# The largest magnitude of a weight strip, spread over the partitions by TensorE and VectorE in place of GpSimd

## The chip, the core and the metric

The kernel runs on one core of one Trainium2 chip. The metric is the device time of one execution in microseconds. Engines are named as in the profile: PE is TensorE's products, PEld its weight loads, DVE is VectorE, ACT is ScalarE, POOL is GpSimd and SP is the engine that only issues DMAs.

## The reference

One inference step of a decoder trunk of two layers, width 1024: a state-space layer and a gated linear recurrence, each followed by a feed-forward layer. There are 1040 prompt tokens (16 of them meta tokens) and 8 sample tokens. Norms, convolutions and recurrences stand around the products; the products with weights carry the arithmetic:

```python
h = rms_norm(x, p["norm_mix_pre"][i])
m, c_new, s_new = ssd_mixer(h, ...)     # or rglru_mixer
x = x + rms_norm(m, p["norm_mix_post"][i])
h = rms_norm(x, p["norm_ffn_pre"][i])
x = x + rms_norm(sq_relu_mlp(h, p["ffn_w1"][i], p["ffn_w2"][i]), p["norm_ffn_post"][i])

def sq_relu_mlp(x, w1, w2):
    h = jax.nn.relu(x @ w1)
    return (h * h) @ w2
```

All inputs are float32, and the products must come out close to float32.

## The kernel before, in words

**Products in float16 parts.** A float32 operand is scaled by a power of two and split into a high and a low float16 part. A product is three passes on PE: high by high, high by low, low by high. Tokens lie along the free dimension in three chunks of 350, 350 and 348 columns.

**Weights come in strips.** A strip is 1024 rows by 256 columns, 1 MB. `wlane` (L399) walks through a list of 113 strips as a generator, one step per `tick`, beside the products. A strip is loaded by SP into one of two buffers `ws` (`load_strip`, L257). Then `wconv` (L285) makes its scale and its parts:

- `rm`, one number per partition that bounds the strip's values there. For kind a it is a sum of magnitudes that ACT accumulates; for kinds d, h and H it is a VectorE reduction over 2048 columns; for kinds 2 and S VectorE reduces in two halves to `r4`, weighs them and reduces again; kind s takes a column that kind g stored in `gmx`.
- `strip_scale` (L262) takes the largest of the 128 numbers on every partition, `wgb`, by GpSimd's `partition_all_reduce`, and VectorE makes from it, in one-column operations, the power of two (`qw`, `pw`, `sw`) and its inverse `winv`.
- ACT writes the high part into `wh`, VectorE the low part (`split`, L271). For kinds H and S (`sums`, L349) there are also the parts `wp` of some quarters, and GpSimd forms four sums of quarters in place in `ws`, which are then split in turn.
- for the first product of a feed-forward layer `hidden_scale` (L418) makes from `wgb` a scale of the hidden units; it multiplies the bound by 32.0.

**Wide and narrow products.** The state-space layer, the recurrent layer and the first and last products of each feed-forward layer are plain (`bundle`): 24 products of 350 or 348 columns per output tile. In between, the feed-forward products go by Winograd's form (`unit`, L1350): seven products of quarters, of 175 or 174 columns, into four of eight PSUM banks, and VectorE adds them up in `z`. The sums of quarters of activations (`f`, `TT`, `HT`) are made by GpSimd (`input_sums`, `t_sums`). `mm` (L240) hands out the banks in turn, eight in the feed-forward layers, four within the state-space groups.

**What sets the order.** The scheduler of the language orders each engine's instructions from the order in which the kernel issues them and from its own estimate of times; on the chip each engine then runs its row in order, waiting at each instruction for its operands. The first 100 us are an exception: in `start` (L746) the engines `hold` the written order. Most operations pass through the wrapper class `Queue`, so that the profile gives L89 (or L92, in the held part) as the line of nearly all; tiles tell them apart.

Of the kernel before, what the change touches and what calls it, by code (L numbers as in the profile page):

```python
# [11 lines left out]
F16 = mybir.dt.float16  # L12
I32 = mybir.dt.int32
AF = mybir.ActivationFunctionType
OP = mybir.AluOpType
AX = mybir.AxisListType
PSUM = bass.MemoryType.PSUM
DRAM = bass.MemoryType.DRAM
# [3 lines left out]
P = 128  # L22
D = 1024
KT = 8
# [29 lines left out]
def cols(c):  # L54
    """The columns of a chunk of tokens."""
    return slice(c * CW, c * CW + WC[c])


class Carve:
    """Small float32 tiles cut from larger ones."""  # L60
# [17 lines left out]
class Queue:  # L78
    """An engine; while hold is set its instructions are issued in program order, and later ones behind them."""
# [38 lines left out]
class Body:  # L118
# [7 lines left out]
    # ------------------------------------------------------- order of work  # L126
    def tick(self):
        """One step of every piece of work that runs beside the matrix products."""
        for lane in list(self.lanes):
            if next(lane, self) is self:  # L130
                self.lanes.remove(lane)
# [5 lines left out]
    def tab(self, *args, **kw):  # L137
        """An activation whose function needs a table set: these stay in program order."""
        if self.last_tab is None or self.nc.scalar.hold:
            self.last_tab = self.nc.scalar.activation(*args, **kw)  # L140
        else:
            with self.tc.issue_after(self.last_tab.ins):
                self.last_tab = self.nc.scalar.activation(*args, **kw)
# [8 lines left out]
    # ---------------------------------------------------------------- setup  # L152
    def setup(self):
# [28 lines left out]
        # pre-norm gains and group-norm gains scaled by a power of two so that hi/lo fit float16  # L182
# [13 lines left out]
        # the inputs of the ffn leave room for sums of four  # L196
# [48 lines left out]
    def pow2(self, b, n, pool, tag):  # L245
        """p = the power of two at or below b; s = 2^14 / p."""
# [9 lines left out]
    # -------------------------------------------------------------- weights  # L256
# [5 lines left out]
    def strip_scale(self, gmax):  # L262
        nc, ty = self.nc, self.tiny
        gb = ty.tile([P, 1], F32, tag="wgb", name="wgb")
        nc.gpsimd.partition_all_reduce(gb, gmax, P, RED.absmax)
        s, p = self.pow2(gb, 1, ty, "w")
        inv = ty.tile([P, 1], F32, tag="winv", name="winv", bufs=8)
        nc.vector.tensor_scalar(inv, p, 2.0 ** -14, None, op0=OP.mult)
        return s, inv, gb

    def split(self, w, st, s, parts):  # L271
        """w = float16 hi and lo parts of st * s, s [P, parts] by contiguous column ranges."""
# [12 lines left out]
    def wconv(self, st, kind, cols=SW):  # L285
        """A strip of weights as float16 hi and lo parts [P, 2, KT, cols], the factor that undoes its scaling and,
        for kinds h and H, the factor of its hidden units. Kind a takes a bound from the sums of the magnitudes, kind s
        one that kind g found before; kinds 2 and S carry the factors of the hidden rows. Kinds H and S are for the
        products by Winograd's form: with the quarters that are used as they are."""
# [50 lines left out]
    def quarter(self, s, inv):  # L340
        """Scales that leave room for sums of four."""
# [7 lines left out]
    def sums(self, wp, st, s, npair, parts):  # L349
        """Steps: the quarters of a strip [K tiles, M] that are used as they are, A11, A12, A22 (A ij: m tile i, k  # L350
        tiles of parity j), as float16 parts in wp; then the sums of Winograd's form in the room of the strip. Only
        the first npair pairs of k tiles."""
# [20 lines left out]
    def product(self, ps, i, w, B, T, npair):  # L373
        """ps = one of the seven products of quarters over the first pairs of k tiles, three passes of the float16
        parts; open for the products of the other pairs where there are any."""
# [14 lines left out]
    def quadrant(self, w, B, npair, i, l):  # L390
        """The operands of m tile i by half l of the tokens over the other pairs."""
# [26 lines left out]
    def hidden_scale(self, wmax, inv):  # L418
        """The factors of one strip's hidden units: t = 2^7, or 2^6 where the squares are summed, / (power of two at or
        below the bound on the values before the square, the norm of the input times that of a column); returns  # L420
        t / (scales of the product); 1 / t^2 goes to rj."""
# [6 lines left out]
        nc.vector.tensor_scalar(lb, wmax, self.gbound[:, gi:gi + 1], 32.0, op0=OP.mult, op1=OP.mult)  # L428
# [14 lines left out]
    def summed(self, b, s):  # L443
        """Whether the hidden units of a strip of block b enter the second product by Winograd's form."""
        return b < 3 and s < NSUM
# [6 lines left out]
    def bundle(self, ps, w, m, act, c, kts=range(KT), first=True, last=True):  # L452
        """ps += sum over k of w[k, m tile]^T act[k, chunk c], three passes of the float16 parts."""
# [14 lines left out]
    def new_u(self):  # L468
        """Float16 parts of the normed input by chunk and k tile."""
# [4 lines left out]
    def u_rows(self, U, c):  # L474
        """The bytes of chunk c of U as float32 rows."""
        return U[:, c].bitcast(F32).rearrange("p k s c -> p k (s c)")

    # ---------------------------------------------------------------- norms
    def rstd(self, sumsq, n, pool, w):
        """1 / sqrt(mean + eps) on every partition, from per-partition sums of squares."""  # L480
# [17 lines left out]
    def normed(self, x, ss, i, hi, lo, pool):  # L498
        """Steps: the pre-norm i of a chunk (its k tiles in x), as float16 parts in hi and lo [P, KT, n]."""
# [15 lines left out]
    def boundary(self, m, ss, xc, piece, ipost, xdst, ipre, U, pool):  # L515
        """Steps: x + norm(m) for a piece of a chunk to xdst; then its pre-norm."""
# [37 lines left out]
    def last_phase(self, ws, act, ipost, xsrc, xdst, ipre, evac, pre=None, split0=None):  # L554
        """The last product before a norm, chunk by chunk; the norms of a chunk run beside the next one."""
# [47 lines left out]
    def first_phase(self, strips, act, evac):  # L603
        """Products of the first strips after a norm: chunk 2 of the input comes last."""
# [15 lines left out]
    # ------------------------------------------------------------------ SSD  # L620
# [67 lines left out]
    def start_x(self, c):  # L688
        """A chunk of the input, in the room of later rows: its k tiles, and room left over."""
# [25 lines left out]
    def start_norm(self, U, c, x, sq, ufs):  # L715
        """Steps: the first pre-norm of a chunk."""
# [29 lines left out]
    def start(self, U):  # L746
        """The first pre-norm beside the first products, issued in this order."""
# [20 lines left out]
    def dt_phase(self, U, dts, dtt, w):  # L768
        """Step sizes, decays and their cumulative sums, tokens on partitions: columns (tile, head); tiles 0-7
        are the chunks of the prompt, 8 the meta tokens, 9 the sample tokens."""  # L770
# [31 lines left out]
        # the sums again, tokens along the rows, in DRAM, from where they are spread over the partitions  # L802
# [22 lines left out]
        # sample tokens  # L825
# [3 lines left out]
        # head rows by sample, then spread over the partitions of the features  # L829
# [13 lines left out]
    def softplus(self, out, x, pool, n, parts=1):  # L843
        """max(x, 0) + log1p(exp(-|x|)), the logarithm by the series of 2 artanh(e / (2 + e)); by parts of the
        columns that don't wait for each other."""
# [23 lines left out]
    def evac_ext(self, pre, ps, c, inv, bias=0.0):  # L869
        """A chunk of projected columns into the layout of the convolution: 8 x (3 state + 1), 3 zeros, tokens."""  # L870
# [10 lines left out]
    def conv_tile(self, pre, out, w4, b1, cvo):  # L881
        """Depthwise convolution of width 4; the last three columns of each sequence go to cvo [P, 27]."""
# [16 lines left out]
    def proj_x(self, g, start=False):  # L899
        """Projection and convolution of the x, B and C columns of a group."""  # L900
# [84 lines left out]
    def ssd_group(self, g):  # L985
# [26 lines left out]
        def spread(i):  # L1012
            """The cumulative sums of a chunk's tokens on every partition."""
# [68 lines left out]
        def sample_bc():  # L1082
            """B and C of the sample tokens, by way of DRAM, on every partition."""
# [22 lines left out]
        def sample_b(b2):  # L1106
            """Two sample tokens: h += x B and y = h C, B and C spread over the partitions."""
# [45 lines left out]
    def group_norm(self, g):  # L1153
        """Steps: gate, norm within the group, float16 parts."""
# [25 lines left out]
    def half_a(self):  # L1180
        """The first half of the output projection, kept in DRAM by chunks."""
# [43 lines left out]
    # ------------------------------------------------------------------ FFN  # L1225
    def ffn(self, l):
# [8 lines left out]
        for b in range(4):  # L1235
# [3 lines left out]
            def square(c, s, r):  # L1239
                """The squares of r (m tile, half of the tokens) as float16 parts, and their sums."""  # L1240
# [78 lines left out]
    def t_sums(self, f, t1, t234):  # L1319
        """Steps: the sums of quarters of the right operand for Winograd's form, in their room in f (B jl: k tiles of  # L1320
        parity j, half l of a chunk's tokens, the last half first): T1 = B12 - B11, T2 = B22 - T1, T3 = B22 - B12,
        T4 = B21 - T2, and their float16 parts."""
# [9 lines left out]
    def input_sums(self, U, TT, fp):  # L1332
        """Steps: the sums of quarters of the input, T1 in the room of B12 and the others in TT."""
# [16 lines left out]
    def unit(self, w, BT, c, npair, fp):  # L1350
        """Two m tiles by a chunk, [C12, C11, C22, C21] (C il: m tile i, half l of the tokens, the last half first), the
        first pairs of k tiles by Winograd's form: seven products of quarters."""
# [27 lines left out]
    # ------------------------------------------------------------------ LRU  # L1380
    def lru(self):
# [99 lines left out]
        # a bound on |h gate|: (32.3 max|x| + max|h0|) (norm of u times that of a column of weights + max|b|)  # L1481
# [74 lines left out]
def _strips(w, ns):  # L1556
    """[K, N] as [ns, 128, (K / 128) * (N / ns)], each strip contiguous per partition."""
# [4 lines left out]
def _fm(x):  # L1562
    """[..., n * 128] as [128, n, ...]"""
# [95 lines left out]
```

## Time and profile before

| | us |
|---|---|
| median of 3 runs | 2842.84 (2841.06 to 2843.44) |
| span of the profiled execution | 2836.7 |
| PE busy in it | 2583.1 |
| VectorE busy | 2110.1 |
| ScalarE busy | 1322.6 |
| GpSimd busy | 691.4 |

The profiled execution's own time isn't listed apart from the runs; its span, from the first instruction to the last, is 2836.7 us, and the three runs lie 4.4 to 6.7 us above it. In the profile's rows `x` is a count; the number in brackets, or behind the bar in groups, is the time that the engine stood idle just before, with what ended it. "issue" there means that nothing in the profile was being waited for.

### The profile page before, as it was taken

How to read it: one execution, taken by the hardware profiler on the slowest of the kernel's cores; microseconds unless marked ns; L12 is line 12 of the kernel's file. 1: busy time of each engine (PE TensorE's matmuls, PEld its weight loads, DVE VectorE, ACT ScalarE, POOL GpSimd, SP SyncE). 2: the span in 40 equal slices, each digit the busy share in tenths (PEclk: the TensorE clock that was granted, in tenths of full speed). 3: DMA queues.
4: the chain of work that ended last, by engine and by line, in shares of the span. 5: the costliest groups of instructions: out<-in, count | busy, mean ns of one | idle time of the engine just before them, and what ended most of it. 6: DMA issues, size and time to landing. Idle time of an engine off the chain costs nothing. (4 is left out here: it accounts for less than half of the span.)

```text
span 2836.7 us, 56933 instructions
## 1 busy us (share of the span) xinstructions
PE 2583.1 (91%) x23209; PEld 2060.6 (73%) x23209; DVE 2110.1 (74%) x5043; ACT 1322.6 (47%) x2148; POOL 691.4 (24%) x972
## 2 busy tenths in 40 slices
PE   4999999999999999789989999979999779989998
PEld 2666666666666667789989976646667779989976
DVE  4889778977873685568778788787685667878776
ACT  4655455545544354344253344658564335253352
POOL 2222111212212024442232201123014452231301
PEclk9999999999999999889999999989999989999999
DMA  3232233223345320101122123110220101111122
GB/s 123 99 119 90 87 107 115 102 88 108 113 159 187 117 106 31 46 31 46 61 72 79 46 110 113 63 62 33 89 108 31 46 31 46 47 45 53 54 73 95
DMA packets 52758, 229.15 MB, mean 81 GB/s; under 512 B 9056, under 2 KB 18416, under 8 KB 31632
## 3 DMA queue, kind: packets, MB, share of 16 engines
q1 hardware_dynamic: 46112, 190.81, 19.1%
q0 software_dynamic: 6384, 34.71, 3.1%
q8 instruction: 181, 2.97, 0.4%
q14 instruction: 81, 0.66, 0.1%
HBM read 186.28 MB, written 39.22 MB: 79 GB/s over the span
## 5 line engine op out<-in xcount | busy, mean ns | idle before, releaser
L89 PEld LDWEIGHTS <-wh 128*128 128x128 f16 x17040 | 1504.0, 99 | 503.7 <-issue 54.7
L89 PE MATMUL mm<-U,wh 128*128 128x350 f16 (+3 forms) x7056 | 989.4, 297 | 20.7 <-ACT rr L89 13.2
L89 PE MATMUL mm<-H,wh 128*128 128x175 f16 (+5 forms) x5664 | 557.7, 253 | 35.3 <-DVE z L89 30.4
L89 PEld LDWEIGHTS <-wp 128*128 128x128 f16 x3888 | 311.0, 99 | 87.6 <-issue 60.5
L89 POOL TENSOR_TENSOR ws<-ws 128x256 f32<-128x256 f32 (+1 forms) x192 | 205.2, 1069 | 328.6 <-DVE wp L89 214.4
L89 DVE TENSOR_TENSOR z<-z,mm 128x175 f32<-128x175 f32 (+3 forms) x648 | 228.4, 370 | 29.2 <-ACT z L89 22.0
L89 POOL PARTITION_ALL_REDUCE wgb<-rm x100 | 55.5, 555 | 656.6 <-issue 338.4
L89 PE MATMUL mm<-U,wp 128*128 128x175 f16 (+1 forms) x1728 | 154.8, 245 | 55.2 <-DVE z L89 55.1
L89 PE MATMUL mm<-TT,wh 128*128 128x175 f16 (+1 forms) x1728 | 167.0, 248 | 10.2 <-ACT TT L89 9.3
L89 ACT ACTIVATE z<-z,ti 128x700 f32<-128x700 f32 (+1 forms) x72 | 63.0, 875 | 183.5 <-DVE z L89 183.5
L89 DVE SCALAR_TENSOR_TENSOR wh<-ws,sw,wh 128x1024 f16<-128x1024 f32 x94 | 122.0, 1320 | 28.3 <-ACT wh L89 28.3
L89 DVE TENSOR_SCALAR qw<-wgb 128x1 f32<-128x1 f32 x103 | 15.5, 150 | 167.3 <-POOL wgb L89 167.1
L89 DVE SCALAR_TENSOR_TENSOR wh<-ws,s,wh 128x256 f16<-128x256 f32 x256 | 114.7, 490 | 11.1 <-ACT wh L89 11.1
L89 DVE TENSOR_REDUCE rm<-ws 128x1 f32<-128x2048 f32 x40 | 91.3, 2281 | 31.2 <-DMA ws<-w 26.7
L89 PE MATMUL mm<-H,wp 128*128 128x175 f16 (+1 forms) x864 | 90.5, 241 | 25.5 <-DVE z L89 23.1
L89 DVE TENSOR_TENSOR ss<-ss,sqt 128x350 f32<-128x350 f32 (+3 forms) x154 | 75.9, 500 | 41.8 <-ACT sqt L89 41.1
L89 ACT ACTIVATE wh<-ws,s 128x512 f16<-128x512 f32 x128 | 83.0, 710 | 48.0 <-POOL ws L89 23.2
L89 DVE SCALAR_TENSOR_TENSOR conv<-pre,ssmall,conv 128x1072 f32<-128x1072 f32 x78 | 103.8, 1330 | 0.1
L89 ACT ACTIVATE wh<-ws,sw 128x2048 f16<-128x2048 f32 x47 | 93.7, 1993 | 14.5 <-DVE sw L89 11.7
L89 DVE TENSOR_SCALAR L<-L,ncs 128x128 f32<-128x128 f32 (+1 forms) x288 | 90.6, 357 | 13.2 <-DMA L<-csd 13.2
L89 DVE TENSOR_TENSOR H<-z,H 128x175 f16<-128x175 f32 (+5 forms) x120 | 81.2, 694 | 23.6 <-ACT H L89 19.5
L89 ACT ACTIVATE pre<-mm,undo 128x8 f32<-128x8 f32 (+1 forms) x104 | 46.5, 474 | 110.7 <-PE mm L89 110.7
(279 smaller groups left out, 4176.9 us busy)
## 6 DMA issues: line engine op xcount, KB each, us to landing
ws<-w SPq DMA_DIRECT2D x64, 1024.0 KB, 4.9
ws<-w_ssd_in SPq DMA_DIRECT2D x24, 1024.0 KB, 5.4
L<-csd SPq DMA_DIRECT2D x64, 256.0 KB, 3.2
ws<-w_lru_in SPq DMA_DIRECT2D x12, 1024.0 KB, 4.9
xd<-xc POOLq DMA_DIRECT2D x6, 1400.0 KB, 5.5
xc<-xd SPq DMA_DIRECT2D x6, 1400.0 KB, 6.0
h<-ssd_h SPq DMA_DIRECT2D x8, 1024.0 KB, 4.9
bc<-bcd SPq DMA_DIRECT2D x8, 1024.0 KB, 4.8
```

The lines of the kernel that those rows point to most:

```text
L89: r = f(*args, **kw)
```

## The change

In `strip_scale` the call on GpSimd goes. In its place PE multiplies: the stationary operand is the upper half of `rm` as bfloat16 (its float32 bytes without the last 16 bits), repeated over 128 columns, and the moving operand is the identity, also as bfloat16. Each output partition then holds all 128 numbers in a row, in a PSUM bank from `mm`, and VectorE reduces that row by its maximum. The bits that are cut off make the maximum smaller by up to 1 in 128, and the bound in `hidden_scale` takes 32.3 in place of 32.0. 109 all-reduces are replaced so; the two others, of the norms' gains (`gb`) and of a bound in the recurrent layer (`gx`), stay on GpSimd. Comments were removed too, so line numbers move by up to five: L89 and L92 become L90 and L93.

```diff
+BF16 = mybir.dt.bfloat16
...
     def strip_scale(self, gmax):
         nc, ty = self.nc, self.tiny
+        ps = self.mm()
+        nc.tensor.matmul(ps[:, :P], gmax.bitcast(BF16)[:, 1:2].to_broadcast([P, P]), self.ident.bitcast(BF16)[:, 1::2], start=True, stop=True)
         gb = ty.tile([P, 1], F32, tag="wgb", name="wgb")
-        nc.gpsimd.partition_all_reduce(gb, gmax, P, RED.absmax)
+        nc.vector.tensor_reduce(gb, ps[:, :P], axis=AX.X, op=OP.max)
         s, p = self.pow2(gb, 1, ty, "w")
...
-        nc.vector.tensor_scalar(lb, wmax, self.gbound[:, gi:gi + 1], 32.0, op0=OP.mult, op1=OP.mult)
+        nc.vector.tensor_scalar(lb, wmax, self.gbound[:, gi:gi + 1], 32.3, op0=OP.mult, op1=OP.mult)
```

The scheduler also orders every engine anew. Three places show it. On POOL, in the first feed-forward layer, while the activations' sums `f` and the weights' sums `ws` are made, there stood before:

```order
L89 TENSOR_TENSOR f<-U 128x350 x2
L89 TENSOR_TENSOR f<-f 128x175 x2
L89 ISA
L89 ISA wgb<-rm 128x1
L89 ISA
L89 TENSOR_TENSOR f<-f 128x175
```

and now:

```order
L90 TENSOR_TENSOR f<-U 128x350 x2
L90 TENSOR_TENSOR f<-f 128x175 x4
L90 TENSOR_TENSOR ws<-ws 128x2x128 x4
L90 TENSOR_TENSOR f<-U 128x350 x2
L90 TENSOR_TENSOR f<-f 128x175 x4
```

The all-reduce went, and with it the instructions without operands that stood ahead of it and behind it.

On VectorE, at a strip of the second hidden block (`z` adds up products, `H` and `HT` are parts of hidden units), the reduction `rm` over a whole strip stood before among these:

```order
L89 TENSOR_REDUCE rm<-ws 128x1
L89 TENSOR_TENSOR z<-z,mm 128x175
L89 TENSOR_TENSOR H<-z,H 128x175
L89 TENSOR_TENSOR H<-z,H 128x350
L89 TENSOR_TENSOR z<-mm,z 128x2x175
L89 TENSOR_TENSOR z<-z,mm 128x175
L89 TENSOR_TENSOR z<-z,mm 128x2x175
L89 TENSOR_TENSOR z<-z,mm 128x175
L89 TENSOR_SCALAR qw<-wgb 128x1
```

and now among these:

```order
L90 TENSOR_TENSOR z<-z,mm 128x2x175
L90 TENSOR_TENSOR H<-z,H 128x174
L90 TENSOR_REDUCE rm<-ws 128x1
L90 TENSOR_TENSOR HT<-z,HT 128x3x174
L90 TENSOR_TENSOR z<-z,mm 128x175
L90 TENSOR_REDUCE wgb<-mm 128x1
L90 TENSOR_TENSOR z<-z,mm 128x175
L90 TENSOR_SCALAR qw<-wgb 128x1
```

Between `rm` and the use of the maximum there stood five `z` adds; one stands there now, and the reduction of the bank is new. On PE the product with `rm` stands between the products for that `z` add and the next ones.

On SP, in a group of the state-space layer, the weight loads `ws` and the loads `L` of decay sums for VectorE stood before:

```order
L1017 DMA L<-csd 128x512
L259 DMA ws<-w_ssd_in 128x2048 x3
L1017 DMA L<-csd 128x512
L1090 DMA bcd_143<-row 8x256
L1093 DMA bc<-bcd_143 128x2048
L1017 DMA L<-csd 128x512 x6
```

and now:

```order
L1022 DMA L<-csd 128x512
L260 DMA ws<-w_ssd_in 128x2048 x2
L1022 DMA L<-csd 128x512
L1095 DMA bcd_143<-row 8x256
L1098 DMA bc<-bcd_143 128x2048
L1022 DMA L<-csd 128x512 x3
L260 DMA ws<-w_ssd_in 128x2048
L1022 DMA L<-csd 128x512 x2
```

The third weight load moved back by four `L` loads.

## The prediction

> **What bounds the kernel now.** I read the table of busy time first, then the same table by stretches of the program.
>
> ```profile
> span 2836.7 us, 56933 instructions
> PE 2583.1 (91%) x23209; PEld 2060.6 (73%) x23209; DVE 2110.1 (74%) x5043; ACT 1322.6 (47%) x2148; POOL 691.4 (24%) x972
> 0.00:140.00 140.00, 96.68 (x802) 63.92 (x803) 95.92 (x197) 74.19 (x111) 41.79 (x63) 0.95 0.31 111
> 140.00:1094.57 954.57, 914.02 (x6073) 630.62 (x6072) 730.03 (x1949) 469.15 (x733) 188.48 (x314) 0.98 0.32 113
> 1094.57:1668.40 573.83, 508.21 (x6266) 497.15 (x6263) 425.76 (x1058) 230.69 (x405) 179.22 (x233) 0.95 0.16 56
> 1668.40:2166.90 498.50, 472.44 (x3033) 308.67 (x3033) 382.81 (x655) 293.75 (x444) 92.67 (x116) 0.98 0.21 77
> 2166.90:2737.19 570.29, 503.46 (x6267) 493.08 (x6264) 415.54 (x1050) 227.79 (x400) 178.57 (x233) 0.95 0.14 48
> 2737.19:2836.70 99.51, 88.30 (x776) 67.19 (x776) 60.04 (x138) 27.07 (x57) 10.65 (x13) 0.97 0.24 86
> ```
>
> Columns are length, then busy time of PE, PEld, DVE, ACT, POOL, then the granted clock. PE is the bound and is idle for 253.6 us. The densest idle time lies in the first 140 us (43.3) and in the two feed-forward stretches of Winograd units (65.6 and 66.8), where the clock is also lowest, 0.95. The waits say who is late.
>
> ```profile
> POOL wgb L89 <- issue: 338.4, 56, 9.3
> DVE qw L89 <- POOL wgb L89: 167.1, 68, 11.7
> PE mm L89 <- DVE z L89: 113.2, 70, 6.2
> POOL ws L89 <- issue: 96.1, 14, 10.2
> ```
>
> GpSimd stands 338.4 us ahead of 56 of its all-reduces although no operand is missing, 6.0 us each, and 96.1 us ahead of 14 weight sums. VectorE stands 167.1 us in 68 waits for the all-reduce. PE's largest wait is for VectorE's `z` adds, which free its banks. One place of the timeline joins the three (first number start, second duration, bracket the idle time ahead):
>
> ```profile
> 1103.02 0.36 POOL L89 PARTITION_ALL_REDUCE wgb<-rm  x1 [4.56 <-DVE rm L89]
> 1110.35 1.53 POOL L89 TENSOR_TENSOR f<-U 128x350 f32<-128x350 f16 x2 [6.97 <-issue]
> 1111.95 2.35 POOL L89 TENSOR_TENSOR f<-f 128x175 f32<-128x175 f32 x4
> 1113.50 0.42 DVE L89 TENSOR_TENSOR U<-f,U 128x175 f16<-128x175 f32 x1 [6.14 <-ACT U L89]
> 1116.98 2.77 PE L89 MATMUL mm<-H,wh 128*128 128x174 f16 x18 [2.43 <-DVE z L89]
> ```
>
> The call takes 0.36 us; the next ordinary GpSimd operation starts 6.97 us later with nothing awaited. VectorE loses 6.14 us to it, PE 2.43 us. The order rows of POOL above show what stands there. The all-reduce and the operand-less instruction on each side of it go. Rows of operand-less instructions fall from 167 to 7 in the program. I read them as the change of GpSimd's code, since the 6 to 7 us lie exactly there. The Trainium skill (GPSIMD Engine Reference, 4.1 Engine selection) advises GpSimd for reductions along partitions. By its 0.36 us call alone the change would have nothing to gain; the rows on both sides of the call decide against that.
>
> **The change part by part.** *The two unit stretches* hold 12,528 narrow products. What they can run at is shown by slices of 100 us and by undisturbed rows:
>
> ```profile
> 1100.00:1200.00 100.00, 81.50 (x959) 79.49 (x959) 58.02 (x151) 33.06 (x65) 48.05 (x71) 0.91 0.09 33
> 1200.00:1300.00 100.00, 82.75 (x945) 81.08 (x944) 67.80 (x163) 46.14 (x76) 43.92 (x61) 0.87 0.09 33
> 1300.00:1400.00 100.00, 97.38 (x1269) 96.07 (x1267) 81.94 (x213) 33.34 (x65) 22.16 (x24) 1.00 0.16 54
> 1400.00:1500.00 100.00, 85.54 (x1049) 83.30 (x1047) 74.81 (x179) 49.23 (x85) 31.62 (x44) 0.95 0.21 75
> 1500.00:1600.00 100.00, 95.97 (x1235) 93.37 (x1234) 82.46 (x212) 26.28 (x51) 22.04 (x23) 1.00 0.18 65
> 2167.36 0.62 PE L89 MATMUL mm<-HT,wh 128*128 128x175 f16 x6
> 2167.82 0.62 PE L89 MATMUL mm<-H,wh 128*128 128x175 f16 x6
> ```
>
> The floor is 0.46 us for six, 76.7 ns. The good slices give 78.8 (100 us / 1269) and 81.0 ns, and these still contain all-reduces; the bad ones 104 to 106. The stretches together take 573.8 + 570.3 = 1144.1 us, 91.3 ns each. I take 81.5 ns, just above the good slices, because VectorE is already 82% busy in them: 1021.0 us, **-123**. Bounds: -157 at 78.8 ns, -183 at the floor, and the VectorE case under the rivals.
>
> *Added on PE:* 109 products of 128 columns. The trace has no such float16 product. Its bounds:
>
> ```profile
> 77.58 6.15 PE L92 MATMUL mm<-wh,U 128*128 128x32 f16 x240
> 390.18 0.49 PE L89 MATMUL tp<-ident,conv 128*16 128x128 f32 x3
> L89 DVE TENSOR_TENSOR cbm<-cb,tri 128x128 f32<-128x128 f32 x64 | 17.8, 277 | 0.0
> L89 DVE TENSOR_REDUCE rm<-ws 128x1 f32<-128x2048 f32 x40 | 91.3, 2281 | 31.2 <-DMA ws<-w 26.7 <-DMA ws<-w_lru_out 2.5 <-DMA ws<-w_lru_in 1.8
> ```
>
> These are 26 ns at 32 columns and 163 ns for a float32 product with the identity; I take 0.1 us, between them: 64 in the feed-forward layers, most of them in the units, **+6**; 32 in the state-space part, +3; 12 in the recurrent layer, +1; the first strip's lies in the start. *Added on VectorE:* 109 reductions of a bank. A 128x128 operation that reads a bank takes 277 ns: 109 x 0.28 = 30 us, hidden by VectorE's 727 us of idle time; without that cover, its own 30 us. The new wait there is for PE, with the `z` adds queued behind it. The `z` add that stands ahead of the reduction on VectorE waits for PE too, for the product right ahead of the small one or at most twelve ahead, so I add nothing (ends 0 and 64 x 0.92 = 59 us).
>
> *The new wait on PE* is the serious one. The product with `rm` stands in PE's row, and every product behind it waits until VectorE has made `rm`. The tightest place is the one shown above for VectorE, a strip of the second hidden block. The two `z` adds around `rm` are twelve products apart on PE, 0.92 us. VectorE needs some 0.5 for the first, 0.4 for `H` and 2.28 for `rm`, 3.2 us: PE stands 2.3. In the order four strips lie so tight, two have 36 products (2.8 us) and the others 48 and more. I take 4 x 2.3 + 2 x 1 = **+11**.
>
> *The start* is written out by hand, so the moved instructions follow each other in a fixed order:
>
> ```profile
> 20.21 1.37 ACT L92 ACTIVATE U<-uf 128x1400 f16<-128x1400 f32 x1
> 24.54 4.15 POOL L92 TENSOR_TENSOR U<-uf,U 128x1400 f16<-128x1400 f32 x1 [6.95 <-ACT U L92]
> 25.26 0.18 ACT L92 ACTIVATION_READ_ACCUMULATOR wh<-ws 128x1 f32 x1
> 28.74 8.42 PE L92 MATMUL mm<-U,wh 128*128 128x350 f16 x47 [6.65 <-POOL U L92]
> 41.66 6.68 POOL L92 TENSOR_TENSOR ss<-ss,sq 128x350 f32<-128x350 f32 x7 [6.78 <-issue]
> 48.40 1.53 PE L92 MATMUL mm<-ss,ones 128*128 128x350 f32 x2 [11.24 <-POOL ss L92]
> 61.19 5.25 PE L92 MATMUL mm<-U,wh 128*128 128x350 f16 x23 [2.97 <-DVE U L92]
> 66.28 0.75 PE L92 MATMUL mm<-ss,ones 128*128 128x348 f32 x2
> 75.62 0.19 ACT L92 ACTIVATION_READ_ACCUMULATOR wh<-ws 128x1 f32 x1
> ```
>
> GpSimd's `U` can start when ACT is done at 21.6, not 24.5: PE starts at about 25.8, also about when the second strip's `rm` lands (25.4), for which PE now waits first. The sums `ss` end near 32.4, before PE is through with its 47 products at 34.2, so the wait of 11.2 vanishes: 14 us early. Then PE meets the fourth strip's `rm`, made by ACT 9.4 us behind the third sum of squares, with 4.4 us of work in hand, and gives back 5. I take **-10**, between -2 and -17.
>
> *State-space and output stretch* (140 to 1094): PE idles 40.6 us there, mostly behind VectorE. GpSimd's loads reach it at times; I take **-8** (0 to -20), as there PE is already 96% busy. SP's queue also moves, as its order rows show: one of three weight loads now stands later, with three `L` loads behind it instead of seven; I count nothing (ends -8 and +8, one us a group). *Recurrent layer and output:* a full `rm` on VectorE with the reduction close behind it in about ten strips, **+8** (0 to +25). The constant 32.3 for 32.0 and the bank taken from the rotation (seven instead of eight between two uses) I cost at nothing.
>
> Sum: -123 + 6 + 11 - 10 - 8 + 3 + 1 + 8 = -112. The span becomes 2724.7. The runs lie 4.4 to 6.7 us above the span (2841.06 to 2843.44), their median 6.1, so **2731 us**.
>
> **The rivals.** *VectorE becomes the bound.* It works 841.3 us in the unit stretches, with 64 reductions 859. At the 82% of the good slices that is 1048 us: with the 11 us of waits the stretches gain 85, not 106, and the time is 2752; with the upper ends of the start (-2), the state-space stretch (0) and the recurrent layer (+25) as well, 2785. For it: 82% in both good slices. Against: its 167 us of waiting for the all-reduce go. *More comes back:* 78.8 ns give 2697, the floor 2671. For it: the good slices still load code. *No change:* the next thing late is the strip's load, which waits for a free buffer and then takes about 5 us ahead of `rm`; if it sets the pace alone, 2843. Against: the stretch from 1300 runs at 97% with the same loads. That the change leaves the code loads in place is excluded by the order. *Slower:* PE waits for `rm` in order, at every one of the 64 unit strips and 12 of the recurrent layer as at the tight place: 76 x 2.3 = 175 instead of the 19 counted, 2731 + 156 = 2887. It decides from 1.7 us a strip. Against: 48 products and more, 3.7 us, at most strips. The rows of 1100 to 1300 show the clock at 0.87 to 0.91 when PE idles for 17 to 19%, and 1.00 at 3 to 4%. The Trainium skill (TensorE: Matmul & The Clock Gate, A second HAM failure mode: psum-queue depth-cycling) says that frequent short idles of PE alone make its clock swing. By it the 109 waits would cost clock too; the slice at 1500, 4% idle at 1.00, speaks against that at my count.
>
> **How the numbers follow.** Forecast 0.58 (own range 2705 to 2752), VectorE bound 0.17, more back 0.15, no change 0.04, slower 0.06. The range 2675 to 2785 leaves out the last two and part of the third. Faster by over 0.2%, which is about what a measurement here can tell from no change, has 0.90, within it 0.04, slower 0.06.
>
> **What would show it.** Right: no "issue" wait ahead of POOL operations, the stretches of units at 80 to 83 ns a product and a clock of 0.98 or more, the first wide products ending some 10 us earlier. Wrong: a wait "PE mm from DVE rm" of more than 40 us in all; PE's wait for `z` still near 113 us; VectorE above 88% in the units.

## The result, and the profile after

The kernel after takes 2924.84 us (median of 4 runs, 2923.44 to 2928.17), the kernel before 2843.14 (2841.06 to 2843.79). The ratio is 1.0295, with a 95% interval of 1.0276 to 1.0313: slower by 82 us, where 112 us less were forecast. The range of the prediction ended at 2785.

The head of the page of after:

```profile
span 2926.4 us, 56787 instructions
PE 2637.8 (90%) x23318; PEld 2091.0 (71%) x23318; DVE 2189.9 (75%) x5152; ACT 1330.3 (45%) x2148; POOL 672.3 (23%) x863
```

Its busy time by the same stretches as before: the first 140 us, the state-space layer and what follows it, the units of the first layer, the recurrent layer, the units of the second layer, the rest. Columns are length, busy PE, PEld, DVE, ACT, POOL, then the granted clock.

```profile
0.00:140.00 140.00, 99.44 (x789) 63.31 (x790) 97.47 (x196) 74.16 (x110) 44.36 (x57) 0.95 0.32 111
140.00:1101.08 961.08, 922.21 (x6125) 634.99 (x6124) 738.85 (x1969) 471.30 (x731) 179.65 (x282) 0.98 0.32 111
1101.08:1715.62 614.54, 524.70 (x6292) 506.33 (x6290) 453.43 (x1077) 230.54 (x402) 178.22 (x208) 0.92 0.15 50
1715.62:2215.59 499.97, 475.52 (x3052) 309.92 (x3050) 384.80 (x677) 295.10 (x442) 82.84 (x98) 0.99 0.22 79
2215.59:2822.65 607.06, 525.75 (x6292) 508.67 (x6290) 445.69 (x1072) 229.50 (x402) 176.95 (x208) 0.92 0.13 43
2822.65:2926.40 103.75, 90.16 (x779) 67.82 (x776) 69.67 (x166) 29.72 (x61) 10.30 (x12) 0.95 0.29 103
```

The two stretches of units took 573.8 + 570.3 = 1144.1 us and take 614.5 + 607.1 = 1221.6 now: 77.5 of the 89.7 us by which the span grew. 91.3 ns a narrow product became 97.5. Half of it is idle time of PE (132.5 to 171.2 us, +38.7). The other half is PE working longer at these products and the small ones between them (1011.7 to 1050.5, +38.8), with the granted clock at 0.92 instead of 0.95. The other four stretches grew by 12.2 together.

The waits of after, the first row of POOL and three of PE:

```profile
POOL ws L90 <- DVE wp L90: 627.7, 37, 26.6
PE mm L90 <- ACT wh L90: 101.7, 42, 6.8
PE mm L90 <- DVE wh L90: 68.7, 83, 1.9
PE mm L90 <- DVE rm L90: 12.4, 5, 4.6
```

What the change aimed at did go: GpSimd's 338.4 us of "issue" ahead of the all-reduces and VectorE's 167.1 us behind them are no rows any more, and so is PE's wait for `z` (113.2 before). In their place PE waits 101.7 + 68.7 = 170.4 us for the float16 parts of weights, `wh`, which it hardly did before. 169.1 us of it lie in the units, nearly all of PE's 171 us of idle time there. GpSimd's row is of the same kind: its sums `ws` stand 627.7 us (214.4 before) for the parts `wp`, which wait for the scale. PE's wait for `rm` is 12.4 us behind the start, and none of it lies in the units.

One strip shows why. Before, an H strip of the second hidden block: the reduction, the all-reduce, the high part, and the first product with that strip's `wh`:

```profile
1172.45 2.28 DVE L89 TENSOR_REDUCE rm<-ws 128x1 f32<-128x2048 f32 x1
1186.45 0.41 POOL L89 PARTITION_ALL_REDUCE wgb<-rm  x1 [6.27 <-issue]
1215.03 1.99 ACT L89 ACTIVATE wh<-ws,sq 128x2048 f16<-128x2048 f32 x1
1239.52 1.08 PE L89 MATMUL mm<-TT,wh 128*128 128x175 f16 x12
```

After, the same strip, with the steps between:

```profile
1185.49 2.29 DVE L90 TENSOR_REDUCE rm<-ws 128x1 f32<-128x2048 f32 x1 [1.14 <-DMA ws<-w]
1210.60 0.22 PE L90 MATMUL mm<-ident,rm 128*128 128x128 bf16 x1
1214.53 0.28 DVE L90 TENSOR_REDUCE wgb<-mm 128x1 f32<-128x128 f32 x1
1216.26 0.71 ACT L90 ACTIVATE wp<-ws,sq 128x512 f16<-128x512 f32 x1
1223.02 0.74 DVE L90 SCALAR_TENSOR_TENSOR wp<-ws,sq,wp 128x512 f16<-128x512 f32 x1
1223.90 5.30 POOL L90 TENSOR_TENSOR ws<-ws 128x512 f32<-128x512 f32 x4 [2.64 <-issue]
1229.23 2.00 ACT L90 ACTIVATE wh<-ws,sq 128x2048 f16<-128x2048 f32 x1 [2.61 <-POOL ws L90]
1231.29 0.47 PE L90 MATMUL mm<-TT,wh 128*128 128x175 f16 x2 [6.79 <-ACT wh L90]
```

`rm` was ready at 1187.8. The product that spreads it stood in PE's row behind others and ran at 1210.6, 23 us later; VectorE reduced the bank 3.9 us after that, behind its `z` adds. From there the parts, GpSimd's sums and the high part follow one upon the other, and PE, which is through with the strip before, waits 6.79 us. Before, the maximum was known 53 us ahead of the use, with GpSimd's pauses in the chain.

I call the time from the end of `sw` (the scale) to the first product with the strip's `wh` the lead. Matched row by row in the traces, its median over the 48 strips of kinds H and S is 38.6 us before and 10.8 after. `rm` now lies ready for 24.1 us (again a median of the 48) before PE gets to the small product. The last low part of `wh` was done 9.8 us ahead of the first product with it before, and is done 3.1 us behind it now (the product begins on the first parts).

### The profile page after: what moved, and what is told of

The parts are those of the page before. It is cut to its first block, busy times and chain, and to the rows that moved or that the text cites. A ratio compares the mean times of both kernels' runs of the same rounds, so it can differ in the third digit from the quotient of the medians.

```text
span 2926.4 us, 56787 instructions
## 1 busy us (share of the span) xinstructions
PE 2637.8 (90%) x23318; PEld 2091.0 (71%) x23318; DVE 2189.9 (75%) x5152; ACT 1330.3 (45%) x2148; POOL 672.3 (23%) x863
## 5 line engine op out<-in xcount | busy, mean ns | idle before, releaser
L90 PEld LDWEIGHTS <-wh 128*128 128x128 f16 x17040 | 1532.8, 100 | 641.5 <-ACT wh L90 108.8
L90 PE MATMUL mm<-U,wh 128*128 128x350 f16 (+3 forms) x7056 | 1015.8, 301 | 11.6 <-ACT rr L90 10.9
L90 PE MATMUL mm<-H,wh 128*128 128x175 f16 (+5 forms) x5664 | 565.8, 254 | 5.6 <-DVE wh L90 5.3
L90 POOL TENSOR_TENSOR ws<-ws 128x256 f32<-128x256 f32 (+1 forms) x192 | 212.1, 1105 | 680.9 <-DVE wp L90 627.7
L90 PEld LDWEIGHTS <-wp 128*128 128x128 f16 x3888 | 304.8, 98 | 3.0 <-DVE wp L90 2.3
L90 PE MATMUL mm<-TT,wh 128*128 128x175 f16 (+1 forms) x1728 | 193.5, 264 | 120.2 <-ACT wh L90 82.1
L90 DVE TENSOR_TENSOR z<-z,mm 128x175 f32<-128x175 f32 (+3 forms) x648 | 232.9, 372 | 82.0 <-ACT z L90 57.5
L90 DVE SCALAR_TENSOR_TENSOR wh<-ws,s,wh 128x256 f16<-128x256 f32 x256 | 144.3, 608 | 27.9 <-ACT wh L90 27.7
L90 ACT ACTIVATE z<-z,ti 128x700 f32<-128x700 f32 (+1 forms) x72 | 63.2, 877 | 191.6 <-DVE z L90 191.6
L90 PE MATMUL mm<-U,wp 128*128 128x175 f16 (+1 forms) x1728 | 146.8, 240 | 0.0
L90 PE MATMUL mm<-HT,wh 128*128 128x175 f16 (+1 forms) x864 | 101.9, 246 | 43.6 <-DVE wh L90 25.2
L90 DVE SCALAR_TENSOR_TENSOR wh<-ws,sw,wh 128x1024 f16<-128x1024 f32 x94 | 118.0, 1284 | 30.0 <-ACT wh L90 30.0
L90 DVE TENSOR_REDUCE rm<-ws 128x1 f32<-128x2048 f32 x40 | 91.3, 2283 | 46.1 <-DMA ws<-w 42.1
L90 ACT ACTIVATE wh<-ws,s 128x512 f16<-128x512 f32 x128 | 85.6, 712 | 84.5 <-POOL ws L90 70.5
L90 DVE TENSOR_TENSOR H<-z,H 128x175 f16<-128x175 f32 (+5 forms) x120 | 94.0, 800 | 33.3 <-ACT z L90 18.8
L90 ACT ACTIVATE pre<-mm,undo 128x8 f32<-128x8 f32 (+1 forms) x104 | 46.7, 477 | 158.6 <-PE mm L90 158.6
L90 ACT ACTIVATE z<-mm 128x175 f32<-128x175 f32 x144 | 43.7, 304 | 160.2 <-PE mm L90 160.0
L90 DVE SCALAR_TENSOR_TENSOR wh<-ws,sq,wh 128x1024 f16<-128x1024 f32 x48 | 61.6, 1283 | 67.6 <-ACT wh L90 67.6
L90 DVE SCALAR_TENSOR_TENSOR conv<-pre,ssmall,conv 128x1072 f32<-128x1072 f32 x78 | 105.9, 1358 | 0.0
L90 ACT ACTIVATE wh<-ws,sw 128x2048 f16<-128x2048 f32 x47 | 93.8, 1999 | 15.9 <-DVE sw L90 14.1
L90 DVE TENSOR_REDUCE r<-ws 128x2 f32<-128x1024 f32 x64 | 77.0, 1213 | 31.4 <-DMA ws<-w 31.4
L90 DVE TENSOR_TENSOR ss<-ss,sqt 128x350 f32<-128x350 f32 (+3 forms) x154 | 76.5, 504 | 30.0 <-ACT sqt L90 29.3
```

What stands on the lines that cost most here:

```text
L90: r = f(*args, **kw)
```

## The experiments

Theory A: PE is busy nearly all the time and runs its row in the order of the program, so the scale of a strip, which used to be free of PE, is now made when PE gets to the small product. The lead shrinks below what the conversion needs, and PE waits for `wh`. Rivals: B, the added work itself (products, banks, reductions); C, the scheduler's new order elsewhere; D, there was nothing to gain.

**Where the loss lies: the change in the units alone.**

```diff
+        if kind in "HS":
+            ps = self.mm()
+            nc.tensor.matmul(ps[:, :P], gmax.bitcast(BF16)[:, 1:2].to_broadcast([P, P]), ...)
...
+            nc.vector.tensor_reduce(gb, ps[:, :P], axis=AX.X, op=OP.max)
+        else:
...
+            nc.gpsimd.partition_all_reduce(gb, gmax, P, RED.absmax)
```

> The kernel after, but only the 48 strips of kinds H and S (the Winograd units) take their maximum by PE and VectorE; the other 61 keep GpSimd's all-reduce. Theory A (tied: PE runs its row in the order of the program, so a strip's scale now waits for PE's place, the float16 parts come late and PE waits for them; the 48 unit strips lost 7 to 14 us of lead each, the others had more lead than they need): the two unit stretches grew by 77 us, the rest by 13, so about 2843 + 77 = 2920, between 2905 and 2930. Rival B (the added work itself: product, bank and reduction cost the same at each strip): 2843 + 82 x 48 / 109 = 2879. Rival C (the scheduler's new order of the state-space part and of the start is what costs): below 2860.

Measured: 2925.7 us, ratio 1.0325 (1.0294 to 1.0357) to the kernel before. Its unit stretches take 1230.7 us. The whole loss is in these 48 strips; B and C as they were put fall.

**The opposite: the change everywhere else** (the condition turned round).

> The opposite: the 48 unit strips keep GpSimd's all-reduce, the other 61 go by PE and VectorE. Theory A: 2843 + 5 to 13 = 2848 to 2856, PE's largest wait again for VectorE's z adds, not for wh. Rival B: 2843 + 82 x 61 / 109 = 2889. Rival C: above 2890.

Measured: ratio 1.0031 (1.0017 to 1.0045), 9 us. The other 61 strips cost little, as A has it.

**All the added work, with nobody waiting for its result** (on the kernel before).

```diff
         nc.gpsimd.partition_all_reduce(gb, gmax, P, RED.absmax)
+        ps = self.mm()
+        nc.tensor.matmul(ps[:, :P], gmax.bitcast(BF16)[:, 1:2].to_broadcast([P, P]), ...)
...
+        nc.vector.tensor_reduce(side, ps[:, :P], axis=AX.X, op=OP.max)
```

> The kernel before with its 109 all-reduces, and beside each the product with rm into a bank and the reduction of that bank, whose result nobody uses. All added work is there, nothing waits for it but PE's row, the bank and VectorE's row. Theory A: the weights keep their lead, 2843 + 10 for the products and some waits for rm: 2845 to 2870. Rival B (work, banks, PE's waits for rm): 2910 or more.

Measured: 2870.0 us, ratio 1.0126 (1.0099 to 1.0153), 36 us. A gave it 2 to 27 us, B 67 or more; it lies between. It left open how much of the loss is work.

**Only the tie to PE** (on the kernel before; `rm` goes through PE and comes back unchanged).

```diff
+        ps = self.mm()
+        nc.tensor.matmul(ps[:, :1], self.ident, gmax, start=True, stop=True)
+        tied = ty.tile([P, 1], F32, tag="tied", name="tied")
+        nc.vector.tensor_copy(tied, ps[:, :1])
         gb = ty.tile([P, 1], F32, tag="wgb", name="wgb")
-        nc.gpsimd.partition_all_reduce(gb, gmax, P, RED.absmax)
+        nc.gpsimd.partition_all_reduce(gb, tied, P, RED.absmax)
```

> The kernel before, but the all-reduce takes rm by way of PE: a product of the identity with rm (one column) and a VectorE copy back, then GpSimd as before. Values are the same. No reduction of a bank, no bfloat16; only the tie to PE's place is added, and the all-reduce's 6 us behind it. Theory A: slower than the kernel after, since the chain behind PE's place is longer by 6 to 13 us on 48 strips that have no slack left: 2950 to 3500. Rival B or C (the reduction of the bank, the new order of VectorE): 2843 to 2880.

Measured: 3035.3 us, ratio 1.0704 (1.0669 to 1.0739). PE waits for `wh` as in the kernel after, 144.6 us behind ACT and 42.0 behind VectorE, with no reduction of a bank and no bfloat16 in it. Besides, it waits 35.1 us for the copy `tied`, which frees the bank of its small product. The tie alone brings the waits for `wh`; that it is worse than the kernel after is what A expected of the all-reduce behind the tie.

**Neither: every partition scales by its own maximum.** The kernel leaves out the maximum over the partitions.

```diff
-        ps = self.mm()
-        nc.tensor.matmul(ps[:, :P], gmax.bitcast(BF16)[:, 1:2].to_broadcast([P, P]), ...)
...
-        nc.vector.tensor_reduce(gb, ps[:, :P], axis=AX.X, op=OP.max)
+        nc.vector.tensor_scalar(gb, gmax, 1.0, None, op0=OP.mult)
```

> The kernel after without the spreading: wgb is a copy of rm on VectorE, so that every partition scales by its own maximum (this leaves out the maximum over the partitions). No product, no bank, no GpSimd call. It shows what the step costs in all. Theory A: the loads of GpSimd's code are gone and nothing is tied to PE, so the units run near 80 ns a product: 2700 to 2760. Rival D (the code loads were hidden, there was nothing to gain): 2835 or more.

Measured: 2673.8 us, ratio 0.9436 (0.9422 to 0.9450). Its unit stretches:

```profile
1065.61:1576.64 511.03, 485.31 (x6268) 479.32 (x6266) 421.41 (x1071) 224.80 (x398) 165.78 (x202) 0.99 0.18 61
2065.62:2570.73 505.11, 483.55 (x6268) 477.82 (x6266) 411.27 (x1063) 226.04 (x400) 164.59 (x202) 1.00 0.15 52
```

1016.1 us for 12,528 products, 81.1 ns each at a clock of 0.99 to 1.00. The gain was there, even beyond the range that A gave; D falls. One row of pauses stays, though no all-reduce of a strip is left:

```profile
POOL ws L90 <- issue: 131.6, 15, 14.6
```

So the 96.1 us of this row before, which the prediction counted beside the 338.4, are not shown to come from the all-reduces.

**The same, and the product and the reduction beside it, unused** (the run before this one with the lines of the side branch).

> As the run in which wgb is a copy of rm (2674; again each partition scales by its own maximum), and beside it, as in the kernel after, the small product into a bank and the reduction of that bank, whose result nobody uses. Between this and the run with two steps more lead (2829) only the use of the result differs. Theory A: the work, the bank and PE's waits for rm cost some 36 us as on the kernel before, 2700 to 2725; the tie of the scale to PE's place is the larger part of the remaining 155. Rival (work, bank and in-order waits for rm are most of it): 2780 to 2830.

Measured: 2686.3 us, ratio 0.947 (0.9456 to 0.9485). The work costs 13 us where nothing depends on it, less than A's 36. From here to the kernel after it is 2924.8 - 2686.3 = 239 us (ratios 1.0295 and 0.947). The small product stands at the same distance from the first use of `wh` in PE's row, and what differs in the program is only the use of the result. B falls with this. Of the 36 us on the kernel before, 23 are then not the work as such; I did not separate them.

**A bank of its own for the small product.**

```diff
-        ps = self.mm()
+        if len(self.mmtags) == 4:
+            ps = self.mm()
+        else:
+            ps = self.psp.tile([P, 512], F32, tag="st", name="mm")
...
-        alltags = self.mmtags = ["mm0", "mm1", "mm2", "tp", "mm3", "cb", "yo", "st"]
+        alltags = self.mmtags = ["mm0", "mm1", "mm2", "tp", "mm3", "cb", "yo"]
```

> The kernel after; outside the state-space groups the small product has a PSUM bank of its own, and the other products turn through seven. Its place in PE's row is nearly the same (163 and 181 products ahead of the use). Theory A: no gain, 2915 to 2960. Rival B in its form of the bank (the small product waits for a bank that VectorE has yet to read): the lead comes back, below 2870.

Measured: 2914.2 us (2 runs), ratio 1.0284 (1.0255 to 1.0312), no change from 1.0295. PE's wait for ACT's `wh` is 98.8 us. The bank is not it.

**More lead: the scale issued earlier.** The arithmetic is the same in the next four; only the place in the program moves. First, ahead of the wait for room:

```diff
+            scale = self.strip_scale(self.bound(st, kind)) if kind in "HS" else None
             while self.ready and sum(...) + cost > self.ahead:
                 yield
...
-            yield from self.wconv(*staged.pop(i))
+            yield from self.wconv(st, kind, cols, scale)
```

> The kernel after; the bound and the scale of an H or S strip are issued ahead of the wait for room among the ready strips instead of behind it, one to three steps earlier. In PE's row the small product of a strip then stands 253 (H) or 217 (S) products ahead of the first use of its wh, not 163 or 181. Theory A: at 77 ns that is 7 or 3 us more lead against 3 us that were missing: PE's waits for wh (170 us) mostly go, 2750 to 2830, faster than before. Rival B (work and banks) and C (order elsewhere): unchanged, 2910 to 2935.

The kinds are interchanged in this text: 163 and 253 products belong to S, 181 and 217 to H. Measured: 2897.5 us, ratio 1.0223 (1.0204 to 1.0242). Faster than after, but far from the 2750 to 2830 that A gave. The lead shows why: the small product runs 20.4 us ahead of the use instead of 14.4 (medians, worked out as the lead is), but the reduction of its bank only 13.0 instead of 11.9. VectorE's row had not moved with PE's; the result is tied to both rows. Then the scale from inside the conversion of the strip before, at its fourth step (`n` counts the steps, so a smaller `n` is earlier):

```diff
...
+            n = 0
+            for _ in self.wconv(st, kind, cols, scale):
+                n += 1
+                if n == 4 and kind in "HS" and i + 1 < len(self.specs) and self.specs[i + 1][1] in "HS":
+                    pre[i + 1] = self.early(*staged[i + 1][:2])
+                yield
```

> As the one before, and the scale of the next strip is issued from inside the conversion of this one: the small product stands some 360 products ahead of the first use of wh, 28 us. Theory A: at least as fast as with 253 and 217, 2710 to 2790, unless PE now waits for rm in its row, which would show as a wait from DVE rm of more than 40 us. Rival B and C: 2910 to 2935.

Measured: 2862.4 us, ratio 1.0095 (1.0070 to 1.0121): a miss of A's range again, still slower than before. Then `n == 2`:

> As the one with the next strip's scale inside the conversion of this one, two steps earlier still: the small product now stands 430 to 460 products ahead of the first use of wh, 34 us, 6 us more. There rm was ready 17 us before PE reached the product. Theory A: PE's waits for z (120 us there, behind VectorE rows that stood for late float16 parts) shrink, 2780 to 2850. Rival: lead is no longer the matter, the bank and the small products themselves are, as in the run with the unused product (36 us): 2855 to 2875, or slower if PE now waits for rm.

Measured: 2829.1 us, ratio 0.9985 (0.9970 to 1.0000), within A's range and level with the kernel before. And `n == 1`:

> As the run with the scale two steps earlier, one more step: the small product stands 470 to 525 products ahead of the first use of wh. If the lead of the scale alone decides, the row of 163 and 181 (2925), 253 and 217 (2898), 360 (2862), 440 (2829) goes on: 2795 to 2825, clearly below the kernel before. Rival: PE now reaches the product before rm is ready; a wait from DVE rm of more than 40 us and 2830 or more.

Measured: 2756.6 us, ratio 0.9715 (0.9695 to 0.9735): 2.9% faster than the kernel before, with all of the change in it, and below the range that went by lead alone. PE's wait for `rm` is 15.8 us, not the more than 40 of the rival.

Side by side (products: the usual number in PE's row from the small product to the first one with the strip's `wh`, for S and H, counted in the order; lead: median; units: both stretches):

| kernel | products S, H | lead us | units us | time us | ratio |
|---|---|---|---|---|---|
| after | 163, 181 | 10.8 | 1221.6 | 2924.8 | 1.0295 |
| ahead of the wait | 253, 217 | 11.7 | 1186.0 | 2897.5 | 1.0223 |
| step 4 | 368, 350 | 21.9 | 1146.8 | 2862.4 | 1.0095 |
| step 2 | 458, 434 | 28.3 | 1118.9 | 2829.1 | 0.9985 |
| step 1 | 524, 470 | 34.6 | 1060.9 | 2756.6 | 0.9715 |
| unused product | 163, 181 (not waited for) | 44.3 | 1023.4 | 2686.3 | 0.9470 |

Every step of lead gives time. The last step leaves 75 us of span to the unused product: 37 in the units and 37 outside, where the other 61 strips are still tied. From step 4 on PE hardly waits for `wh` (7.0 us behind ACT), yet lead still pays. The waits of VectorE and PE at step 4, step 2 and step 1 suggest how:

```profile
DVE wh L90 <- ACT wh L90: 150.7, 66, 7.0
PE mm L90 <- DVE z L90: 120.2, 81, 4.1
```

```profile
DVE wh L90 <- ACT wh L90: 122.2, 71, 5.4
PE mm L90 <- DVE z L90: 98.8, 82, 5.0
```

```profile
DVE wh L90 <- ACT wh L90: 63.9, 60, 4.5
PE mm L90 <- DVE z L90: 54.4, 42, 3.3
PE mm L90 <- DVE rm L90: 15.8, 8, 4.4
```

With little lead VectorE stands in its row for the high part that ACT has yet to make, the `z` adds queue behind it, and PE waits for the banks. Both fall together.

**Neither PE nor GpSimd: by way of DRAM.**

```diff
+            nc.sync.dma_start(d, gmax)
+            nc.sync.dma_start(row, d[None, :, 0].to_broadcast([P, P]))
+            nc.vector.tensor_reduce(gb, row, axis=AX.X, op=OP.max)
```

> The kernel after, but for the 48 unit strips rm goes to DRAM by a DMA (512 bytes), comes back by a second one spread over the partitions (128 x 128), and VectorE reduces that; the other strips go by PE as before. Neither PE's row nor GpSimd's code is in the chain; two transfers are. Theory A: the lead of the scale over the first use of wh returns from 12 us to 30 or more, units near 81 to 84 ns a product: 2690 to 2760, faster than the kernel before. Rival (VectorE's reduction of 128 columns and its place in VectorE's row are what costs, wherever the numbers come from): 2820 or more.

Measured: 3021.5 us, ratio 1.0673 (1.0649 to 1.0696). A's number fails by far, though the lead is back at 43.8 us; the rival's range holds, and the rows bear out the half of it that speaks of the place in VectorE's row. The longest wait of VectorE in the waits:

```profile
DVE wgb L90 <- DMA rmrow<-rmd: 369.6, 48, 11.0
```

One strip in the timeline, on VectorE and on SP's queue:

```profile
1306.62 0.29 DVE L90 TENSOR_REDUCE wgb<-rmrow 128x1 f32<-128x128 f32 x1 [9.72 <-DMA rmrow<-rmd]
...
1295.25 0.32 SPq L273 DMA_DIRECT2D rmd<-rm  x1
1302.57 0.32 SPq L275 DMA_DIRECT2D rmrow<-rmd  x1
```

From the first issue to the reduction it is 11.4 us, and VectorE stands 7.7 us a strip at the reduction, with the `z` adds behind it: PE's wait for `z` is 180.8 us. That SP's queue stands 330.4 us between the two transfers, ahead of the weight loads, is not seen to cost: VectorE waits 21.1 us for strips ahead of `rm`, against 42.1 in the kernel after. So lead alone does not decide; a long step hurts wherever a row has to stand for it, as VectorE stood 167.1 us for the all-reduce before. In the kernel after VectorE does not wait for the small product in the units (its 23.3 us behind PE lie elsewhere), so this is not what slows that one. I did not try the reduction placed later in VectorE's row.

## Why the prediction was wrong

- **What bounds the kernel, and the -123 us: right, but not to be had this way.** I took 81.5 ns a product for units without GpSimd's pauses. Without the pauses and without a tie they run at 81.1. The forecast time, 2731, lies between the step-1 version and the one with no spreading.
- **The step that failed is "the new wait on PE is the serious one".** I asked only whether PE has to wait for `rm`. I did not ask the reverse, whether the scale has to wait for PE. The sum let the scale follow `rm` at once, as with the all-reduce on an idle engine, and had no term for parts `wh` that come late: it has 1021 + 6 + 11 = 1038 us for the units, and they take 1221.6. That is 184 of the 202 us by which the span missed. PE's row in the order, where the prediction looked only for what stands around `rm`, would have given it: 163 or 181 products of 76.7 ns are 12.5 to 13.9 us, while the conversion from the small product to the last low part takes 17.5 us (14.4 + 3.1, medians). In the trace of before 28.8 us passed from the scale to the last low part (38.6 - 9.8). Against the run with the result unused the tie costs 198 us in the units (1221.6 against 1023.4) and 44 outside (1704.8 against 1661.1).
- **The 11 us for that wait come near the 12.4 measured by luck.** They were counted at six strips of the units, and in the units PE waits for `rm` nowhere. Of the 12.4 us, 3.1 lie in the state-space stretch, 6.8 in the recurrent layer and 2.5 behind the last units. The 8 us for the recurrent layer and the output were right: 9.3.
- **My signs of being wrong did not show.** PE's wait for `rm` stayed under 40 us, its wait for `z` went, VectorE is busy for 74% of the units. The list lacked the same wait as the sum. Of the signs of being right, the time of a product (97.5 ns) and the clock (0.92) failed.
- **The rival on the slower side had the right sign and another mechanism.** It had PE standing at the product with `rm` at every strip, and was argued away with 48 products between two `z` adds. PE stands there five times in the main part and never in the units; there it stands for `wh` instead. 0.06 for slower was too little.
- **Products and reductions added: right.** A reduction takes 285 ns, 29.2 us for 103 in the main part (0.28 was taken). PE goes on 0.06 us after a small product begins (0.1 was taken). VectorE is busy for 74% of the units, so the rival that it becomes the bound did not come; with the result unused it is busy for 82%, as the prediction had it.
- **The start: a third of it; the state-space layer: wrong.** Ten us were to come early out of the start. PE's wait of 11.24 us for `ss` went, but the products of 32 columns begin only 3.1 us earlier (74.48, before 77.58), since PE now waits three times at a small product:

```profile
26.73 0.29 PE L93 MATMUL mm<-ident,rm 128*128 128x128 bf16 x1 [8.25 <-ACT wh L93]
50.88 0.23 PE L93 MATMUL mm<-ident,rm 128*128 128x128 bf16 x1 [3.76 <-ACT wh L93]
65.77 0.29 PE L93 MATMUL mm<-ident,rm 128*128 128x128 bf16 x1 [5.04 <-ACT wh L93]
74.48 6.15 PE L93 MATMUL mm<-wh,U 128*128 128x32 f16 x240
```

ACT's sum of magnitudes, which makes `rm` there, writes through `wh`. I had put such a wait at nothing for the second strip, had none for the third, and had 5 us for the fourth, which came so. With the result unused the three waits stay (16.9 us): here PE does wait for `rm` in its row, as I had looked for it in the units. Eight us were to come out of the state-space stretch; it ends 6.5 us later, at 1101.1. With the result unused the units begin at 1071.3, 30 us earlier; at the products of 32 columns it is only 1.7 us ahead. So behind the start it is the tie and not the work that takes the time.
- **The clock.** I wrote that by the Trainium skill (TensorE: Matmul & The Clock Gate, A second HAM failure mode: psum-queue depth-cycling) frequent short idles would cost clock as well, and held against it that the waits I counted were few. The rows agree: 0.92 where PE idles for 13 to 15% of the units, 0.99 to 1.00 where it idles for 4 to 5% (no spreading). The half of the loss in the units in which PE is busy goes with it: 1011.7 us at 0.95 would be some 1045 at 0.92, an estimate from these rows, and 1050.5 were measured. That the short idles pull the clock down is the rule of the Trainium skill; no run here changes them alone.

The Trainium skill (TensorE: Matmul & The Clock Gate, the table at its head) calls the queues of ScalarE, VectorE and GpSimd strict first-in, first-out. VectorE's `z` adds queued behind the reduction in the run by way of DRAM agree with that.

## What to carry to other kernels

A step that moves from an idle engine to the busiest one does not only cost its duration there: its result comes when that engine gets to it. Count in the order how many instructions of the bound engine stand between the moved step and the first user of its result, and compare that time with the chain that hangs on it. If it is too short, issue the step earlier in the program; here that turned 2.9% slower into 2.9% faster.

## What was not expected of the hardware

A DMA of 512 bytes from 128 partitions to DRAM took 7.2 us from issue to landing (median of 48), longer than the 4.5 us of the 64 KB that came back and the 4.9 us of a 1 MB strip in the same run. The Trainium skill (DMA: Bandwidth & Descriptors, Anatomy of one DMA — SWDGE (gpsimd) path) fits 2.0 us and a term by bytes to DMAs that GpSimd issues, which would make an estimate of 2.0 us for 512 bytes. This one was issued by SP, which that fit does not cover, and took three and a half times as long.

Leaving out one reduction over partitions per strip, 0.41 us of a call, was worth 160 us of 2834: with the call went GpSimd's pauses of 6 to 7 us on both sides of it and the waits of VectorE and PE behind them. What GpSimd does in the pauses stays open. I read them as loads of its code, but the two DMA queues that the page of the profile lists as instruction queues moved 2.97 and 0.66 MB in the kernel before and just as much in the run with no spreading.
